# The queue that writes split weight parts back to memory: SyncE's, or GpSimd's where GpSimd makes the lo part

## The chip, the core and the metric

The kernel runs on one core of a Trainium2 chip. The metric is the device time of one execution in microseconds (us). Engines are named as in the profile: PE (TensorE matmuls), PEld (its weight loads), DVE (VectorE), ACT (ScalarE), POOL (GpSimd) and SP (SyncE, which here only issues DMAs). "SPq" is the queue of SP's instructions.

## What is computed

One layer of a decoder trunk over 2048 prompt tokens and 8 sample tokens of width 1024, in float32. Cut to its shape:

```python
h = rmsnorm(x, g_mix) * (1 + scale_m) + shift_m          # modulation from c @ w_ada
q, k, v, g_ret, x_lru, g_lru = split(h @ w_in)           # 1024 x 3072
ret_out = silu(g_ret) * norm(retention(rot(q), rot(k), v))
lru_out = rg_lru(causal_dwconv(x_lru)) * gelu(g_lru)
x = x + gate_m * (concat(ret_out, lru_out) @ w_out)      # 1024 x 1024
h = rmsnorm(x, g_ffn) * (1 + scale_f) + shift_f
u, gv = h @ w_up_conv, h @ w_up_gate                     # 1024 x 2816 each
x = x + gate_f * ((gelu(causal_dwconv(u)) * gv) @ w_down)  # 2816 x 1024
y = rmsnorm(x, g_final)
```

States of the retention, the recurrence and the two convolutions are outputs too.

## The kernel before

**Tiling.** The tokens are cut into three groups (688, 680 and 680 + 8), and each group into two blocks of 340 or 344 columns. A group runs through the layer's stages in turn: projection with retention and recurrence, output projection, then the up, gate and down products. The up and gate products are done for pairs of 128 output columns (pairs 0 to 10) with seven products for eight (`quad_item`), so their left operands are blocks of the weights (A11, A12, A22) or sums of them (S1 to S4).

**Split weights.** A float32 product is made of three fast ones: hi x hi, hi x lo and lo x hi (`mm3`, L373 to L375; only L375 reads a weight's lo part). So each weight block of 128 x 512 is split in a tile `wb` of 128 x 1024: ACT copies it rounded into the first half (L303), and POOL or DVE (`lo_on`, L304) subtracts that to fill the second. This is done when a key (a weight block's name) comes up for the first time. The whole tile, 512 KB, is then written to a DRAM tile `split[key]` (L310), and later groups read it back with one load (L301). Keys called `late` are not written the first time, but are split again in the second group and written then.

**Who makes lo.** `fetch(k, lo_on=V if near else G)`: DVE for the upper half of w_out and for pairs 0 to 2 of the up and gate weights, and for the first keys of the program; POOL for the others.

**Order and queues.** The main loop runs over a list of items (one product each) and fetches keys ahead until those that are not yet used weigh 4 (`LOOK`). A scheduler then fixes the order of each engine's instructions ahead of time, from its own model of their cost, and each engine works through its own list in order. Loads of raw weights (`wr`, L281 and L287) share a ring of 7 tiles with the sums `ws` (L357); the blocks `wb` share a ring of 8. In the kernel before, all of these loads and all writes are issued by SP. POOL issues 11 small loads at the start (L183, L246) and no other DMA; its work is lo parts of weights (L304) and of activations (`ffl`, `flast`, `mix`, L458), and small steps of the norms, the rotation and the recurrence. PE reads w_ada's raw tiles directly (L397).

Of the kernel before, what the change touches and what calls it, by code (L numbers as in the profile page):

```python
# [10 lines left out]
F32 = mybir.dt.float32  # L11
# [87 lines left out]
def hybrid_step(ctx: ExitStack, tc: tile.TileContext, I, O):  # L99
    nc = tc.nc  # L100
    V, S, G, T = nc.vector, nc.scalar, nc.gpsimd, nc.tensor
# [166 lines left out]
    split = {}  # L268
# [22 lines left out]
    def late(key):  # L291
        kind, a = key[0], key[1]
        if kind == "w_in":
            t = a // P
            return t % 4 == 3 or t >= 16 and t % 4 == 2 or t < 16 and t % 4 == 0
        return kind == "w_out" and a % 512 >= 2 * P

    def parts(key, w, src=None, lo_on=G):

        if src is None:  # L300
            nc.sync.dma_start(out=w.bitcast(F32), in_=split[key])  # L301
        else:
            S.activation(out=w[:, 0:512], in_=src, func=AF.Copy)  # L303
            lo_on.tensor_tensor(out=w[:, 512:1024], in0=src, in1=w[:, 0:512].bitcast(F32), op=ALU.subtract)  # L304
            nm = "_".join(str(v) for v in key)
            if late(key) and key not in once:
                once.add(key)
                return [w[:, 512 * i:512 * i + 512].rearrange("p (k c) -> p k c", c=P) for i in range(2)]
            split[key] = dp.tile([P, 1024], F32, tag=nm, name=nm)
            nc.sync.dma_start(out=split[key], in_=w.bitcast(F32))  # L310
        return [w[:, 512 * i:512 * i + 512].rearrange("p (k c) -> p k c", c=P) for i in range(2)]

    def fetch(key, r_=None, lo_on=G):

        kind, a = key[0], key[1]
        if kind == "ada01":
            src = I["w_ada"][0, key[2] * P:(key[2] + 1) * P, 0:2 * D].rearrange(
                "p (j c) -> p j c", j=2)[:, :, a * 512:(a + 1) * 512]
            if isinstance(r_, tuple):
                for j in range(2):  # L320
                    nc.sync.dma_start(out=r_[j], in_=src[:, j])
            else:
                nc.sync.dma_start(out=r_.rearrange("p (j c) -> p j c", j=2), in_=src)
                r_ = (r_[:, 0:512], r_[:, 512:1024])
            units[key] = [h[:, c:c + 256] for h in r_ for c in (0, 256)]
        elif kind == "w_ada":
            r_ = [load_rows_of(kind, key[2] * P, a * D + 512 * h) for h in range(2)]
            units[key] = [r_[h][:, c:c + 256] for h in range(2) for c in (0, 256)]
        elif kind in ("w_down", "w_out"):

            units[key] = parts(key, block(), None if key in split else load_rows_of(kind, a, 512 * key[2]), lo_on)
        elif kind == "w_in":
            both = []
            for h in range(2):
                r_ = None if key + (h,) in split else load_cols_of(kind, a, h)
                both.append(parts(key + (h,), block(), r_, lo_on))
            units[key] = [(both[k // 4][0][:, k % 4, :], both[k // 4][1][:, k % 4, :]) for k in range(KC)]
        else:
            fetch_operand(key, lo_on)

    def fetch_operand(key, lo_on):


        kind, i, nm = key
        if key in split:
            units[key] = parts(key, block())
            return
        pr = pairs.setdefault((kind, i), {})

        def A(n):  # L350
            if n not in pr:
                pr[n] = load_cols_of(kind, P * (2 * i + int(n[1]) - 1), int(n[2]) - 1)
            return pr[n]

        def total(n, x, y, op):
            pr[n] = rtile("ws")
            V.tensor_tensor(out=pr[n], in0=x, in1=y, op=op)  # L357

        if nm == "S1":
            total("S1", A("A21"), A("A22"), ALU.add)  # L360
            total("S2", pr["S1"], A("A11"), ALU.subtract)
        elif nm == "S2":
            total("S4", A("A12"), pr["S2"], ALU.subtract)
        elif nm == "S3":
            total("S3", A("A11"), A("A21"), ALU.subtract)
        units[key] = parts(key, block(), A(nm) if nm[0] == "A" else pr[nm], lo_on)
        if (i == 1 or i == 2 and kind == "w_up_conv") and nm in ("A11", "A12"):

            del pr[nm]
# [1083 lines left out]
```

## Time and profile before

| | |
|---|---|
| median of 3 runs | 2460.2 us (2459.76 to 2463.95) |
| the profiled execution | 2463.86 us, its span 2462.1 us |
| mean granted TensorE clock | 0.988 |
| SP's main queue (q1) | 532.01 MB, 62.6% of the 16 DMA engines' span |
| DMAs issued by POOL (q0) | 0.56 MB, 0.1% |
| weight blocks written (L310) | 262 of 512 KB each, all on SP |
| lo parts made by POOL (L304) | 228 |

The page gives busy times of the engines, the chain of work that ended last, and groups of instructions by line. A line number names the instruction's place in the kernel: L303 hi, L304 lo, L310 the write, L301 the load of a written block. A row "A <- B" of the view of waits says that engine A's instruction stood until B's ended. The stage views show the same numbers for stretches of the span.

### The profile page before, as it was taken

Reading aid. Unit: us, or ns where it says so; the run is one execution under the profiler, and the core shown is the slowest. Engines: PE = TensorE matmul, PEld = TensorE weight load, DVE = VectorE, ACT = ScalarE, POOL = GpSimd, SP = SyncE. Lnnn points to the kernel's source line nnn. Section 1 sums busy time; section 2 is a strip of 40 time slices with the busy share of each in tenths; the row PEclk is TensorE's granted clock in tenths of the full one; section 3 lists DMA queues with packets and bytes.
Section 4 is the critical chain, followed back from the end, with each engine's and each line's share of the span. In section 5 each row is a group of like instructions: output and inputs, shape, how many; then the busy total and the mean of one; then the engine's idle time right before and its main releaser. Section 6 shows DMA issues by size and latency. Waiting matters only on the chain.

```text
span 2462.1 us, 40114 instructions
## 1 busy us (share of the span) xinstructions
PE 2359.8 (96%) x15157; PEld 2275.5 (92%) x15157; DVE 1452.9 (59%) x3181; ACT 869.6 (35%) x1964; POOL 716.9 (29%) x739
## 2 busy tenths in 40 slices
PE   5999998999999999999899999999999989999998
PEld 4987797999999999999899999999999989999998
DVE  5646777875766665666754444446667675444444
ACT  4323554544444444243422222243124241222222
POOL 3444440257666743243001010112222210101011
PEclk9999999999999999999999999999999999999999
DMA  9476655878878875343566666666442465666674
GB/s 299 163 261 223 210 172 190 305 276 287 304 285 304 323 251 184 120 157 139 189 222 235 222 238 220 241 213 215 139 130 96 145 231 199 239 220 234 219 252 160
DMA packets 243493, 536.04 MB, mean 218 GB/s; under 512 B 19223, under 2 KB 114055, under 8 KB 243292
## 3 DMA queue, kind: packets, MB, share of 16 engines
q1 hardware_dynamic: 242220, 532.01, 62.6%
q8 instruction: 120, 1.97, 0.3%
q10 hardware_dynamic: 696, 0.91, 0.1%
q0 software_dynamic: 384, 0.56, 0.1%
q14 instruction: 73, 0.60, 0.1%
HBM read 385.10 MB, written 148.42 MB: 217 GB/s over the span
## 4 chain that ended last, share of the span: by engine, by line
PE 53%; DVE 4%; ACT 2%; DMA 1%; issue 1%; POOL 1%; POOLq 0%; SPq 0%; ACTq 0%; DVEq 0%
PE down L374 6%; PE down L373 6%; PE down L375 6%; PE qx L374 4%; PE qx L375 4%; PE qx L373 4%; PE proj L373 3%; PE proj L375 3%; PE proj L374 3%; PE qz L373 2%; PE qz L374 2%; PE qz L375 2%; PE qy L374 1%; PE qy L373 1%; PE qy L375 1%
## 5 line engine op out<-in xcount | busy, mean ns | idle before, releaser
L851 DVE SCALAR_TENSOR_TENSOR x<-down,mod,x 128x344 f32<-128x344 f32 (+2 forms) x624 | 349.0, 569 | 347.0 <-PE down L375 342.3
L373 PE MATMUL proj<-hh,wb 128*128 128x344 f32 (+1 forms) x1152 | 378.5, 329 | 14.3 <-DVE h L580 6.0
L375 PE MATMUL proj<-hh,wb 128*128 128x344 f32 (+1 forms) x1152 | 373.6, 325 | 2.7 <-POOL wb L304 2.5
L374 PE MATMUL proj<-hl,wb 128*128 128x344 f32 (+1 forms) x1152 | 372.5, 323 | 0.0
L458 POOL TENSOR_TENSOR ffl<-cv,ffh 128x344 fp32r<-128x344 f32 (+1 forms) x120 | 124.7, 1046 | 782.0 <-ACT ffh L457 736.7
L374 PE MATMUL qx<-op,wb 128*128 128x344 f32 (+1 forms) x1020 | 325.5, 319 | 2.6 <-DVE op L921 2.6
L373 PE MATMUL qx<-op,wb 128*128 128x344 f32 (+1 forms) x1020 | 324.7, 320 | 1.2 <-ACT op L920 1.2
L375 PE MATMUL qx<-op,wb 128*128 128x344 f32 (+1 forms) x1020 | 324.5, 319 | 0.0
L373 PE MATMUL down<-ffh,wb 128*128 128x344 f32 (+1 forms) x960 | 304.7, 324 | 7.6 <-DVE x L851 7.4
L375 PE MATMUL down<-ffh,wb 128*128 128x344 f32 (+1 forms) x960 | 306.4, 319 | 0.0
L374 PE MATMUL down<-ffl,wb 128*128 128x344 f32 (+1 forms) x960 | 306.3, 319 | 0.0
L304 POOL TENSOR_TENSOR wb<-wr,wb 128x512 fp32r<-128x512 f32 x164 | 223.9, 1376 | 230.7 <-ACT wb L303 222.1
L373 PEld LDWEIGHTS proj<-hh,wb 128*128 128x128 f32 x1152 | 218.4, 190 | 25.9 <-issue 9.5
L375 PEld LDWEIGHTS proj<-hh,wb 128*128 128x128 f32 x1152 | 218.7, 190 | 5.7 <-POOL wb L304 3.9
L374 PEld LDWEIGHTS proj<-hl,wb 128*128 128x128 f32 x1152 | 219.1, 190 | 3.3 <-POOL hl L588 0.9
L1076 DVE SCALAR_TENSOR_TENSOR cv<-u,vec,cv 128x344 f32<-128x344 f32 (+2 forms) x264 | 170.8, 665 | 50.6 <-ACT cv L1056 48.1
L374 PEld LDWEIGHTS qx<-op,wb 128*128 128x128 f32 x1020 | 191.7, 188 | 3.4 <-DVE op L921 3.4
L373 PEld LDWEIGHTS qx<-op,wb 128*128 128x128 f32 x1020 | 191.5, 188 | 2.0 <-ACT op L920 1.8
L373 PEld LDWEIGHTS down<-ffh,wb 128*128 128x128 f32 x960 | 179.3, 188 | 14.3 <-DVE x L851 13.7
L375 PEld LDWEIGHTS qx<-op,wb 128*128 128x128 f32 x1020 | 191.4, 188 | 0.0
L373 PE MATMUL qz<-op,wb 128*128 128x344 f32 (+1 forms) x528 | 169.7, 325 | 14.6 <-ACT op L920 10.7
L375 PEld LDWEIGHTS down<-ffh,wb 128*128 128x128 f32 x960 | 180.6, 188 | 0.0
(314 smaller groups left out, 4952.1 us busy)
## 6 DMA issues: line engine op xcount, KB each, us to landing
wb<-w_down SPq DMA_DIRECT2D x100, 512.0 KB
wb<-w_up_conv_S SPq DMA_DIRECT2D x92, 512.0 KB
wb<-w_up_gate_S SPq DMA_DIRECT2D x92, 512.0 KB
wb<-w_in SPq DMA_DIRECT2D x72, 512.0 KB
wb<-w_up_conv_A SPq DMA_DIRECT2D x69, 512.0 KB
wb<-w_up_gate_A SPq DMA_DIRECT2D x69, 512.0 KB
w_in<-wb SPq DMA_DIRECT2D x48, 512.0 KB
w_up_conv_S<-wb SPq DMA_DIRECT2D x44, 512.0 KB
```

The lines of the kernel that those rows point to most:

```text
L304: lo_on.tensor_tensor(out=w[:, 512:1024], in0=src, in1=w[:, 0:512].bitcast(F32), op=ALU.subtract)
L373: T.matmul(out, wh, xh, start=first, stop=False, skip_group_check=more)
L374: T.matmul(out, wh, xl, start=False, stop=False, skip_group_check=more)
L375: T.matmul(out, wl, xh, start=False, stop=last, skip_group_check=more)
L458: G.tensor_tensor(out=lo[:, 0:n], in0=src, in1=hi[:, 0:n].bitcast(F32), op=ALU.subtract)
L851: V.scalar_tensor_tensor(out=xs, in0=q[:, 0:np_], scalar=modv[:, jg, m, 0:1], in1=xs, op0=ALU.mult, op1=ALU.add)
L1076: V.scalar_tensor_tensor(out=cv[:, 0:np_], in0=u[:, j:j + np_], scalar=cfw[:, j, ft:ft + 1], in1=cv[:, 0:np_], op0=ALU.mult, op1=ALU.add)
```

## The change

```diff
             split[key] = dp.tile([P, 1024], F32, tag=nm, name=nm)
-            nc.sync.dma_start(out=split[key], in_=w.bitcast(F32))
+
+            (nc.gpsimd if lo_on is G else nc.sync).dma_start(out=split[key], in_=w.bitcast(F32))
         return [w[:, 512 * i:512 * i + 512].rearrange("p (k c) -> p k c", c=P) for i in range(2)]
```

The write of a split block is issued by POOL where POOL makes the lo part, and by SP as before where DVE makes it. The added blank line moves all lines behind it down by one: in the kernel after, the write is L311, `mm3` L374 to L376 and the activations' lo L459.

Of 262 writes, 212 move to POOL: 48 of w_in, 8 of w_out, 56 of w_up_conv, 56 of w_up_gate and 44 of w_down. The 50 others stay on SP. Since the scheduler places all instructions again, the order on the other engines moves too: PE's from its 428th row to the second group's projections, and not behind them (on ACT two small steps change places near the end).

The order on SP, in the projections of the first group (the place at 205 to 226 us of the profile before). `wr` are raw weight tiles, `w_in_0_2281` is the DRAM tile of a key's first half. Before:

```order
L287 DMA wr<-in_w_in 128x4x128 x2
L287 DMA wr<-in_w_up_conv 128x4x128
L310 DMA w_in_0_2281<-wb 128x1024
L281 DMA wr<-in_w_ada 128x512 x2
L310 DMA w_in_1_2288<-wb 128x1024
L310 DMA w_up_conv_S_2332<-wb 128x1024
L287 DMA wr<-in_w_in 128x4x128 x2
L281 DMA wr<-in_w_ada 128x512 x2
L310 DMA w_in_0_2347<-wb 128x1024
```

The same place in the change:

```order
L287 DMA wr<-in_w_in 128x4x128 x2
L287 DMA wr<-in_w_up_conv 128x4x128
L281 DMA wr<-in_w_ada 128x512 x2
L287 DMA wr<-in_w_in 128x4x128
L311 DMA w_up_conv_S_2332<-wb 128x1024
L287 DMA wr<-in_w_in 128x4x128
L281 DMA wr<-in_w_ada 128x512 x4
```

The loads keep their order. The three writes of w_in are gone from between them, and the write of w_up_conv's S, whose lo part DVE makes, stays and now stands between the two w_in loads.

The order on POOL, in the feed-forward of the first group (at 646 to 660 us of the profile before), where the lo parts of pair 6 and of w_down are made. Before:

```order
L304 TENSOR_TENSOR wb_7209<-wr_7185,wb_7209 128x512
L458 TENSOR_TENSOR ffl_7133<-cv_6845,ffh_7132 128x344
L304 TENSOR_TENSOR wb_7231<-ws_7229,wb_7231 128x512
L304 TENSOR_TENSOR wb_7236<-ws_7187,wb_7236 128x512
L458 TENSOR_TENSOR ffl_7158<-cv_6884,ffh_7157 128x344
L304 TENSOR_TENSOR wb_7249<-wr_7250,wb_7249 128x512
L458 TENSOR_TENSOR ffl_7182<-cv_6948,ffh_7181 128x344
L304 TENSOR_TENSOR wb_7286<-wr_7287,wb_7286 128x512
L304 TENSOR_TENSOR wb_7332<-wr_7107,wb_7332 128x512
L304 TENSOR_TENSOR wb_7369<-wr_7370,wb_7369 128x512
```

In the change, from three writes behind wb_7209 on:

```order
L311 DMA w_up_conv_6_S2_7192<-wb_7189 128x1024
L304 TENSOR_TENSOR wb_7231<-ws_7229,wb_7231 128x512
L304 TENSOR_TENSOR wb_7236<-ws_7187,wb_7236 128x512
L304 TENSOR_TENSOR wb_7249<-wr_7250,wb_7249 128x512
L311 DMA w_up_conv_6_A12_7212<-wb_7209 128x1024
L304 TENSOR_TENSOR wb_7286<-wr_7287,wb_7286 128x512
L311 DMA w_up_conv_6_S3_7234<-wb_7231 128x1024
L311 DMA w_up_conv_6_S4_7239<-wb_7236 128x1024
L311 DMA w_down_1280_1_7254<-wb_7249 128x1024
L304 TENSOR_TENSOR wb_7332<-wr_7107,wb_7332 128x512
L311 DMA w_down_1408_1_7291<-wb_7286 128x1024
L304 TENSOR_TENSOR wb_7369<-wr_7370,wb_7369 128x512
```

The lo parts keep their order; between wb_7209 and wb_7369 there are now eight writes (two of w_down stand ahead of the rows shown), one to three lo parts behind the part that they write.

The order on PE at the product that reads wb_7369 (the gate's A11 of pair 6), with its first lo matmul as the third row of that product. Before:

```order
L375 MATMUL qz_7214<-op_4274,wb_7236 128x344
L373 MATMUL qx_7490<-op_4006,wb_7369 128x344
L374 MATMUL qx_7490<-op_4006,wb_7369 128x344
L375 MATMUL qx_7490<-op_4006,wb_7369 128x344
L373 MATMUL qx_7490<-op_4006,wb_7369 128x344
L374 MATMUL qx_7490<-op_4006,wb_7369 128x344
L373 MATMUL down_7316<-ffh_7101,wb_7136 128x344
```

In the change:

```order
L375 MATMUL down_7467<-ffl_7182,wb_7286 128x344
L376 MATMUL down_7467<-ffh_7181,wb_7286 128x344
L374 MATMUL qx_7490<-op_4006,wb_7369 128x344
L375 MATMUL qx_7490<-op_4006,wb_7369 128x344
L374 MATMUL qz_7526<-op_4194,wb_7413 128x344
L375 MATMUL qz_7526<-op_4194,wb_7413 128x344
L374 MATMUL down_7475<-ffh_7101,wb_7249 128x344
```

The product starts 45 rows further back in PE's list, and its first lo matmul 83 rows further back, behind down products and a part of pair 6's A22 that stood after it before.

## The prediction

> **What bounds the kernel now.** The page's head and its chain of waits come first, then the busy time of the engines by stage. Columns of the stage rows: stretch in us, its length, busy time (and instructions) of PE, PEld, DVE, ACT and POOL, granted TensorE clock, share of the DMA engines, GB/s.
>
> ```profile
> span 2462.1 us, 40114 instructions
> PE 2359.8 (96%) x15157; PEld 2275.5 (92%) x15157; DVE 1452.9 (59%) x3181; ACT 869.6 (35%) x1964; POOL 716.9 (29%) x739
> PE 53%; DVE 4%; ACT 2%; DMA 1%; issue 1%; POOL 1%; POOLq 0%; SPq 0%; ACTq 0%; DVEq 0%
> 60.00:180.00 120.00, 120.00 (x808) 106.87 (x808) 64.54 (x179) 37.56 (x71) 52.77 (x59) 1.00 0.64 212
> 180.00:310.00 130.00, 120.58 (x771) 99.31 (x770) 90.20 (x165) 55.72 (x98) 58.13 (x58) 0.99 0.66 215
> 450.00:860.00 410.00, 400.00 (x2506) 392.40 (x2505) 283.08 (x421) 188.35 (x429) 254.46 (x195) 1.00 0.82 296
> 1260.00:1630.00 370.00, 370.00 (x2386) 369.94 (x2385) 159.83 (x305) 94.73 (x243) 37.16 (x38) 1.00 0.68 235
> ```
>
> TensorE is busy for 96% of the span, and no other engine has more than 4% of the chain. So a change to queues pays only where PE stands still for a weight. All the moved writes lie in group 0, apart from 24 of the late w_in keys, whose parts are made again and written in group 1. The stage rows show three kinds of stretch. From 60 to 180 us PE never stops (120.00 of 120.00), although the writes are already being made. From 180 to 310 us it stands still for 9.4 us. From 450 to 860 us, the feed-forward of group 0, where most of the writes lie, it stands still for 10 us of 410. The same work in group 1 (1260 to 1630 us), where split weights are only read back, has no gap.
>
> Next, what PE waited for in 180 to 310 us, and in 450 to 860 us (the last two rows). Columns: engine, line, waited for; total us, times, longest.
>
> ```profile
> PE proj L373 <- ACT wb L303: 2.9, 2, 1.9
> PE proj L375 <- POOL wb L304: 2.5, 2, 2.1
> PE zr L816 <- DVE xc L807: 2.5, 1, 2.5
> PE ada L397 <- DMA wr<-in_w_ada: 0.6, 2, 0.4
> PE down L373 <- ACT wb L303: 0.3, 1, 0.3
> PE down L373 <- DVE x L851: 7.4, 19, 1.6
> PE down L374 <- POOL flast L458: 1.6, 2, 0.9
> ```
>
> In 450 to 860 us PE waits for a PSUM bank that DVE has to drain (7.4 us), never for a weight part. Weights are late only in 180 to 310 us: 2.9 + 2.5 + 0.6 + 0.3 us, and the 2.5 us for the recurrence chain stand behind a late projection. The row for POOL's wb reads the same over the whole span, so the 24 writes of group 1 hold no PE wait either and count as 0.
>
> **What goes: writes that hold SP.** SP issues in order, so a load behind a write stands until the lo part is made. The waits of SP, over the whole span (first row) and in 180 to 310 us, and how long POOL's own DMA issues take by line (last three rows: instruction ns, min/median/max):
>
> ```profile
> SPq L310 <- POOL wb L304: 344.7, 155, 18.9
> SPq L281 <- DVE ws L357: 17.0, 3, 11.1
> SPq L281 <- PE ada L397: 16.3, 8, 4.6
> SPq L310 <- POOL wb L304: 16.1, 5, 4.9
> SPq L310 <- DVE wb L304: 8.0, 4, 2.8
> SPq L287 <- POOL wb L304: 6.9, 5, 2.5
> SPq L287 <- PE ada L397: 5.6, 2, 4.6
> SPq L281 <- POOL wb L304: 4.1, 3, 3.6
> L183 POOL DMA_DIRECT2D rows<-in_state_ffn_conv x3: 526/539/558, 4.5 to 5.5; - x3
> L246 POOL DMA_DIRECT2D wri<-in_w_r x2: 653/662/670, 6.1 to 6.7; - x2
> L183 POOL DMA_DIRECT2D rows<-in_conv_ffn_w x1: 772/772/772, 1.6 to 1.6; - x1
> ```
>
> The 344.7 us are the time for which SP stood at a write whose lo part POOL had not finished; these waits leave SP. Most of them hide nothing from PE, since the lo parts stand several products ahead. In 180 to 310 us the seven waits listed come to 74.0 us, of which the moved writes have 16.1, or 22%. The others stay: a load that waits for a slot of the seven raw tiles (for ws, ada or wb), and the writes whose lo part DVE makes (8.0 us), which remain on SP and stand in front of the same loads. The weight waits of PE with the recurrence are 8.8 us, and the clock of 0.99 over 130 us costs 1.3 us more, 10.1 us in all. The gain's upper end is therefore 10 us, if every one of them hangs on the writes, and its share by SP's waits is 22% of 10.1 = 2.2 us. I take **-2 us**, because one place can be followed on SP's timeline (start, length, engine, line, transfer) and PE's:
>
> ```profile
> 212.81 0.34 SPq L310 DMA_DIRECT2D w_in<-wb  x1
> 213.25 1.21 SPq L281 DMA_DIRECT2D wr<-in_w_ada  x2
> 215.08 0.38 SPq L310 DMA_DIRECT2D w_up_conv_S<-wb  x1
> 215.52 2.67 SPq L287 DMA_DIRECT2D wr<-in_w_in  x2
> 222.42 0.43 PE L373 MATMUL proj<-hh,wb 128*128 128x344 f32 x1 [1.03 <-ACT wb L303]
> ```
>
> The write at 212.81 is the one that SP waited for (longest 4.9 us); the w_in loads that PE lacks at 222.42 go out 2.7 us later. Without it they can move up, and this 1.0 us goes, but the write at 215.08 has a lo part from DVE and still stands between the two. Where this wait goes, the raw slots are late next. The other direction is open too: an lo part that PE takes at once (the two waits of 2.5 us) comes later by each write that POOL issues first. I allow one write ahead of each of the five waits for parts (2 + 2 + 1 times), 5 x 0.54 us, 3 us lost.
>
> The Trainium skill (DMA: Bandwidth & Descriptors, "Issuing engines are not separate DMA queues") says that transfers from any engine run on the same 16 DMA engines and that spreading the issue saves only sequencer time. Taken alone, that makes the change worth 212 issues on SP and nothing on PE, a term of 0 for my -2; the row of 344.7 us shows a wait in order that this rule does not count.
>
> **What comes: 212 issues on POOL.** POOL's own DMA issues are in the trace, in its first 9 us: 0.53 to 0.56 us for 128 rows, 0.65 to 0.67 for the larger pattern, 0.77 for the first. A write of a block has 128 rows, so I take **0.54 us**. All 212 cost 114 us of POOL, which has 1745 us free in the span. What counts is where they lie: 156 of them (44 of w_down, 112 of the up and gate operands of pairs 3 to 10) are in 450 to 860 us. There POOL goes from 254.5 to 254.5 + 84.2 = 338.7 us of 410, from 62% to 83%. It is not full, but its work comes in bursts, here on POOL's timeline, with the product that needs the last part:
>
> ```profile
> L304 POOL TENSOR_TENSOR wb<-wr,wb 128x512 fp32r<-128x512 f32 x90 | 125.8, 1411 | 89.2 <-ACT wb L303 84.7 <-DVE x L851 3.4 <-DMA wr<-in_w_in 0.9
> L304 POOL TENSOR_TENSOR wb<-ws,wb 128x512 fp32r<-128x512 f32 x64 | 91.2, 1431 | 56.4 <-ACT wb L303 45.2 <-DMA w_up_conv_A<-wb 11.1
> 649.85 2.83 POOL L304 TENSOR_TENSOR wb<-ws,wb 128x512 fp32r<-128x512 f32 x2
> 652.63 0.94 POOL L458 TENSOR_TENSOR ffl<-cv,ffh 128x344 fp32r<-128x344 f32 x1
> 653.51 1.30 POOL L304 TENSOR_TENSOR wb<-wr,wb 128x512 fp32r<-128x512 f32 x1
> 654.76 0.94 POOL L458 TENSOR_TENSOR ffl<-cv,ffh 128x344 fp32r<-128x344 f32 x1
> 655.64 4.26 POOL L304 TENSOR_TENSOR wb<-wr,wb 128x512 fp32r<-128x512 f32 x3
> 661.77 0.32 PE L375 MATMUL qx<-op,wb 128*128 128x344 f32 x1
> ```
>
> The last of the three at 655.64 is wb_7369 and ends at 659.90; its first lo matmul is the one at 661.77, so 1.87 us are to spare. In POOL's new order eight writes stand between wb_7209 and wb_7369: 8 x 0.54 = 4.3 us. In the old PE order that is 2.4 us late, and over the eight pairs 3 to 10 19 us: the upper end. But PE's order changes as well: that lo matmul is 83 rows further back, at 400 us / 2506 = 0.16 us each 13 us later, behind work on parts that are older. So I take **+1 us**, near the lower end of 0: no weight part was waited for in this stage, and in the two rows above POOL itself stands idle for 145.6 us at these parts, mostly for ACT's hi part, which the earlier loads can only bring forward. If that cover is gone the 19 us come. What is queued behind a write on POOL is the next lo part or the lo half of an activation (ffl), for which PE waits; the write itself waits for the lo part ahead of it on the same engine, and for its queue's eighth write before. Where that one has not landed, POOL stands; writes lie about 2.6 us apart (410/156), so eight are 21 us, against 6.5 to 7.7 us to landing:
>
> ```profile
> DMA to landing us min/median/max: 6.5/6.8/7.7
> L357 DVE TENSOR_TENSOR ws<-wr 128x512 f32<-128x512 f32 x37 | 39.5, 1067 | 61.5 <-DMA wr<-in_w_up_gate 51.2 <-POOL wb L304 9.6 <-DMA wr<-in_w_up_conv 0.6
> ```
>
> The first row is that of the four wri loads of POOL. The bytes moved are the same, and a block is written again only after PE has used it, so a write that lands a few us later delays no one at 0 us; its bound is the same 19 us.
>
> **The sum.** -2 + 1 = -1 us. The profiled execution took 2463.9 us (span 2462.1), 3.7 us over the median of the three timed runs, 2460.2; taken from its own time that is 2462.9, and a median run should again lie some 3.7 us lower. I forecast **2459 us**. A measurement of this kernel can tell about 0.2%, 4.9 us, from no change.
>
> **Rivals.**
> - *SP runs free*: all weight waits of 180 to 310 us go, with the clock: 2460.2 - 10 = 2450. For it speak the 344.7 us; against it, the 57.9 of 74.0 us of SP waits that stay there.
> - *POOL fills up* (slower): in 450 to 860 us a write holds POOL twice as long as in its quiet start, 1.08 us; 254.5 + 168.5 = 423 us do not fit into 410, and PE waits for lo parts: +13, 2473. It decides from 155.5 us free / 156 = 1.00 us per write on, and hurts earlier where bursts run over. For it: the lo parts there take 1411 and 1431 ns on average, so POOL is already slowed beside DVE. Against it: 0.54 against 1.00.
> - *DVE holds up POOL's DMA issues*: each write waits for one DVE instruction of 1.07 us before its 0.54; 156 x 1.61 = 251 us against 155.5 free, +96, 2556. The Trainium skill (SBUF — State Buffer, "SBUF: two separate sides") describes such a lock against descriptors made on GpSimd, for DVE instructions that use both ports on one source, 620 ns becoming about 3100. The row above is a two-input form, so I give it little.
> - *Nothing changes places*: SP only waits for raw slots instead, and POOL's issues hide: 2460, inside the forecast.
>
> **How the numbers follow.** Forecast with the last rival 0.48, SP free 0.26, POOL full 0.23, the lock 0.03. The forecast's own spread crosses 4.9 us once in fifty on either side: faster 0.26 + 0.01 = 0.27, same 0.46, slower 0.23 + 0.03 + 0.01 = 0.27. The range takes the ends of the terms, 2460.2 - 10 = 2450 and 2460.2 + 19 = 2479; the lock stays outside, and the forecast's own range is 2455 to 2465.
>
> **What would show it.** Right: SP's wait at L310 for POOL's wb is all but gone, its waits on raw slots (ws, ada) have grown; POOL's busy time is about 831 us, a write at 0.5 to 0.7 us; PE's weight waits of 180 to 310 us are 2 us fewer, and PE still waits for no lo part in 450 to 860 us. Wrong: a median issue near 1 us on POOL with PE waiting for POOL's wb (slower), or PE without weight waits from 180 to 310 us (faster).

## The result, and the profile after

| | before | after |
|---|---|---|
| median of 4 runs each | 2461.7 us (2459.8 to 2464.0) | 2501.5 us (2500.2 to 2504.8) |
| ratio after / before | | 1.0169, 95% interval 1.0155 to 1.0183 |
| span of the profiled execution | 2462.1 us | 2503.1 us |

The change costs 40 us. The forecast was 2459 us with a range up to 2479, so the time lies outside it, on the slower side.

The head of the page after:

```profile
span 2503.1 us, 40095 instructions
PE 2369.3 (95%) x15157; PEld 2283.1 (91%) x15157; DVE 1485.3 (59%) x3181; ACT 879.2 (35%) x1969; POOL 823.6 (33%) x951
```

POOL has 212 instructions and 107 us more than before, close to what was forecast. What was not forecast is DVE: the same 3181 instructions take 1485.3 us instead of 1452.9.

Four stages of the kernel after, each cut at the count of PE's matmuls that the kernel before reaches at 60, 180, 310, 450 and 860 us (columns as in the prediction):

```profile
60.60:187.30 126.70, 121.91 (x808) 106.86 (x808) 66.12 (x179) 37.39 (x73) 67.06 (x82) 0.98 0.62 208
187.30:312.00 124.70, 120.04 (x772) 100.93 (x771) 86.62 (x165) 53.51 (x95) 60.73 (x66) 0.99 0.63 207
312.00:455.30 143.30, 124.56 (x770) 119.78 (x770) 110.67 (x242) 76.54 (x168) 39.67 (x46) 0.96 0.60 202
455.30:903.30 448.00, 412.02 (x2507) 401.58 (x2506) 305.46 (x413) 190.82 (x428) 322.88 (x341) 0.97 0.74 266
```

The last row is the feed-forward of group 0. It took 410 us before and takes 448.0 for as many matmuls (2507, one more at an edge): 38 of the 40 us. PE stands still for 36.0 us instead of 10.0, and its matmuls take 412.0 us instead of 400.0, because the granted clock is lower (0.97 against 1.00): around six stops of 2.0 to 4.3 us the trace has stretches of 3.4 or 6.8 us at half the clock (0.50 in 621.0 to 624.4 us, for one). The stage before has no stop over 1.6 us and no such stretch. Of the rest, 60 to 180 us before takes 6.7 us more, 180 to 310 us takes 5.3 us less, 310 to 450 us 3.3 us more. Behind it, 860 to 1260 us takes 3.3 us less, and the feed-forward of group 1 takes the same 370 us.

What PE waits for in that stage after (the chief rows):

```profile
PE qz L374 <- ACT wb L303: 12.5, 9, 3.7
PE qx L374 <- ACT u L1017: 11.4, 5, 4.3
PE down L374 <- DVE x L852: 5.1, 7, 1.1
PE qx L374 <- ACT p L1017: 3.0, 1, 3.0
```

PE waits for no lo part of POOL, as the prediction said. It waits for hi parts of ACT and for PSUM banks that ACT drains, neither of which it waited for there by more than 0.2 us before. The reader should not stop at ACT: it is the last of a chain. The sums `ws` of the weight parts, which DVE makes, by line in the kernel before (instruction ns, min/median/max) and who waited for them (us, times):

```profile
L357 DVE TENSOR_TENSOR ws<-wr,ws x22: 676/694/1780, 214.5 to 827.5; 128x512 f32<-128x512 f32 x22
...
  ACT wb L303: 9.3, 10
```

The same view of the kernel after:

```profile
L358 DVE TENSOR_TENSOR ws<-ws,wr x22: 674/688/4280, 210.0 to 871.7; 128x512 f32<-128x512 f32 x22
L358 DVE TENSOR_TENSOR ws<-wr,ws x22: 675/1260/5545, 220.8 to 872.7; 128x512 f32<-128x512 f32 x22
...
  ACT wb L303: 41.6, 20
```

The shortest sums take 0.67 to 0.68 us in both kernels. Before, the longest took 1.8 us; after, 5.5 us, and ACT waits 41.6 us for sums instead of 9.3. Not only sums are held: the convolution steps of L1104 take up to 4.0 us and those of L1077 up to 3.7, against 1.6 and 1.7 before. One such place, on the timeline of the kernel after: the longest sum on DVE and the sum behind it, then POOL beside it.

```profile
609.65 5.54 DVE L358 TENSOR_TENSOR ws<-wr,ws 128x512 f32<-128x512 f32 x1
615.12 1.41 DVE L358 TENSOR_TENSOR ws<-wr 128x512 f32<-128x512 f32 x1
609.66 1.29 POOL L304 TENSOR_TENSOR wb<-ws,wb 128x512 fp32r<-128x512 f32 x1
610.91 0.91 POOL L459 TENSOR_TENSOR ffl<-cv,ffh 128x344 fp32r<-128x344 f32 x1
611.78 0.57 POOL L311 DMA_DIRECT2D w_up_conv_S<-wb  x1
612.37 0.94 POOL L459 TENSOR_TENSOR ffl<-cv,ffh 128x344 fp32r<-128x344 f32 x1
613.27 1.28 POOL L304 TENSOR_TENSOR wb<-wr,wb 128x512 fp32r<-128x512 f32 x1
614.51 1.47 POOL L459 TENSOR_TENSOR ffl<-cv,ffh 128x344 fp32r<-128x344 f32 x1
```

The sum stands while POOL works off four instructions and a write one behind the other at their own pace. The write at 611.78 does not let it in; only the instruction at 614.51 takes longer (1.47 us instead of 0.91 to 0.94), so the sum gets in there, beside an elementwise instruction. What comes of it, on the same timeline for ACT, SP and PE (in brackets the wait ahead of the instruction):

```profile
616.57 1.15 ACT L303 ACTIVATE wb<-ws 128x512 fp32r<-128x512 f32 x2 [3.74 <-DVE ws L358]
616.56 0.83 SPq L281 DMA_DIRECT2D wr<-in_w_down  x2
620.39 0.63 ACT L303 ACTIVATE wb<-wr 128x512 fp32r<-128x512 f32 x1 [2.67 <-DMA wr<-in_w_down]
620.92 0.44 ACT L1017 ACTIVATE u<-qx 128x344 f32<-128x344 f32 x1
617.77 0.42 PE L374 MATMUL qz<-op,wb 128*128 128x344 f32 x1 [1.81 <-ACT wb L303]
621.42 0.66 PE L374 MATMUL qx<-op,wb 128*128 128x344 f32 x1 [3.07 <-ACT u L1017]
```

ACT stands 3.74 us for the sums, and PE 1.81 us for the hi part made of one. The sums also hold raw tiles, so SP's next loads of w_down leave only at 616.56. ACT works in order and stands 2.67 us for that load, with the drain of a PSUM bank behind it, for which PE stands another 3.07 us. These 4.9 us of PE stand behind the held sum and the one queued behind it. How much of them would be left with two short sums is not shown: SP had waited for these tiles since before the hold.

For comparison the timeline of the kernel before, where a sum also starts just behind a lo part: it is let in behind that one part, and the next lo part waits for it (1.75 us instead of 1.28).

```profile
515.97 1.76 DVE L357 TENSOR_TENSOR ws<-wr 128x512 f32<-128x512 f32 x1
515.89 1.29 POOL L304 TENSOR_TENSOR wb<-ws,wb 128x512 fp32r<-128x512 f32 x1
517.14 1.75 POOL L304 TENSOR_TENSOR wb<-wr,wb 128x512 fp32r<-128x512 f32 x1
```

### The profile page after: what moved, and what is told of

It reads as the page before. It is cut to its first block, busy times and chain, and to the rows that moved or that the text cites. A ratio compares the mean times of both kernels' runs of the same rounds, so it can differ in the third digit from the quotient of the medians.

```text
span 2503.1 us, 40095 instructions
## 1 busy us (share of the span) xinstructions
PE 2369.3 (95%) x15157; PEld 2283.1 (91%) x15157; DVE 1485.3 (59%) x3181; ACT 879.2 (35%) x1969; POOL 823.6 (33%) x951
## 4 chain that ended last, share of the span: by engine, by line
PE 53%; DVE 4%; ACT 3%; DMA 2%; issue 1%; POOL 1%; POOLq 0%; SPq 0%; ACTq 0%; DVEq 0%
PE down L375 6%; PE down L374 6%; PE down L376 6%; PE qx L375 4%; PE qx L374 4%; PE qx L376 4%; PE proj L374 3%; PE proj L376 3%; PE proj L375 3%; PE qz L374 2%; PE qz L375 2%; PE qz L376 2%; PE qy L374 1%; PE qy L375 1%; PE qy L376 1%
## 5 line engine op out<-in xcount | busy, mean ns | idle before, releaser
L374 PE MATMUL proj<-hh,wb 128*128 128x344 f32 (+1 forms) x1152 | 379.1, 329 | 17.2 <-DVE h L581 6.0
L459 POOL TENSOR_TENSOR ffl<-cv,ffh 128x344 fp32r<-128x344 f32 (+1 forms) x120 | 125.1, 1050 | 776.2 <-ACT ffh L458 734.9
L376 PE MATMUL proj<-hh,wb 128*128 128x344 f32 (+1 forms) x1152 | 373.0, 324 | 1.2 <-POOL wb L304 1.1
L374 PE MATMUL qx<-op,wb 128*128 128x344 f32 (+1 forms) x1020 | 327.4, 322 | 16.4 <-ACT u L1017 11.4
L376 PE MATMUL qx<-op,wb 128*128 128x344 f32 (+1 forms) x1020 | 325.2, 320 | 0.0
L374 PE MATMUL down<-ffh,wb 128*128 128x344 f32 (+1 forms) x960 | 304.0, 323 | 7.1 <-DVE x L852 6.7
L376 PE MATMUL down<-ffh,wb 128*128 128x344 f32 (+1 forms) x960 | 306.1, 320 | 0.0
L374 PEld LDWEIGHTS proj<-hh,wb 128*128 128x128 f32 x1152 | 218.4, 190 | 27.6 <-issue 8.4
L376 PEld LDWEIGHTS proj<-hh,wb 128*128 128x128 f32 x1152 | 218.5, 190 | 3.8 <-POOL wb L304 2.0
L374 PEld LDWEIGHTS qx<-op,wb 128*128 128x128 f32 x1020 | 192.4, 189 | 20.5 <-ACT u L1017 13.3
L374 PE MATMUL qz<-op,wb 128*128 128x344 f32 (+1 forms) x528 | 171.3, 328 | 26.3 <-ACT wb L303 12.5
L376 PEld LDWEIGHTS qx<-op,wb 128*128 128x128 f32 x1020 | 192.1, 189 | 0.4 <-POOL wb L304 0.4
L1077 DVE SCALAR_TENSOR_TENSOR cv<-u,vec,cv 128x344 f32<-128x344 f32 (+2 forms) x264 | 167.0, 651 | 40.7 <-ACT cv L1057 38.5
L374 PEld LDWEIGHTS down<-ffh,wb 128*128 128x128 f32 x960 | 179.5, 188 | 11.2 <-DVE x L852 10.6
L303 ACT ACTIVATE wb<-wr 128x512 fp32r<-128x512 f32 x206 | 125.3, 625 | 175.1 <-DMA wr<-in_w_in 59.8
```

What stands on the lines that cost most here:

```text
L374: T.matmul(out, wh, xh, start=first, stop=False, skip_group_check=more)
L376: T.matmul(out, wl, xh, start=False, stop=last, skip_group_check=more)
L459: G.tensor_tensor(out=lo[:, 0:n], in0=src, in1=hi[:, 0:n].bitcast(F32), op=ALU.subtract)
L1077: V.scalar_tensor_tensor(out=cv[:, 0:np_], in0=u[:, j:j + np_], scalar=cfw[:, j, ft:ft + 1], in1=cv[:, 0:np_], op0=ALU.mult, op1=ALU.add)
```

## The experiments

Differences are to the median of the kernel before, measured beside it on the same chip. All edits are to `parts`, in the form of the changed line unless said. Every edit gives the scheduler a new order on all engines, which by itself can move the time by some us. The last two columns are from the trace of one run of each kernel: how long the feed-forward of group 0 takes, cut at the same counts of PE's matmuls as 450 and 860 us before, and how many of DVE's instructions in it take over 2 us.

| kernel | median, us | before, us | difference | stage, us | over 2 us |
|---|---|---|---|---|---|
| the kernel before | | | | 410.0 | 0 |
| the change | 2501.5 | 2461.7 | +39.8 | 448.0 | 18 |
| feed-forward's 156 writes on POOL | 2500.4 | 2460.8 | +39.6 | 450.8 | 17 |
| mixing stage's 56 writes on POOL | 2469.3 | 2460.0 | +9.3 | 406.6 | 0 |
| all 212 on ACT's queue | 2479.7 | 2460.8 | +18.9 | 416.2 | 0 |
| feed-forward's 156 on ACT's queue | 2469.8 | 2460.1 | +9.8 | 409.3 | 0 |
| writes on SP, 212 small DMAs on POOL | 2490.6 | 2460.0 | +30.6 | 434.7 | 20 |
| writes on SP, 67 small DMAs on POOL | 2486.3 | 2463.6 | +22.7 | 434.4 | 14 |
| writes on SP, POOL copies, 0.44 us per lo part | 2464.2 | 2460.8 | +3.4 | 412.0 | 0 |
| writes on SP, POOL copies, 0.55 us per lo part | 2468.4 | 2459.4 | +9.0 | 410.1 | 0 |
| writes on SP, POOL copies, 0.77 us per lo part | 2552.6 | 2463.6 | +89.0 | 488.0 | 0 |
| the change, and a small copy behind each write | 2549.3 | 2460.1 | +89.2 | 474.7 | 8 |
| the change with 9 raw tiles and 7 blocks | 2535.8 | 2460.0 | +75.8 | 477.4 | 22 |
| before with 9 raw tiles and 7 blocks | 2450.4 | 2460.1 | -9.7 | 399.1 | 0 |

Every kernel in which POOL issues DMAs among its work in that stage has instructions of DVE over 2 us there, and no other has one (the longest is 1.88 us).

### Where: the two parts of the change alone

```diff
+            (nc.gpsimd if lo_on is G and key[0] not in ("w_in", "w_out") else nc.sync).dma_start(...)
```

> Only the 156 writes of w_down, w_up_conv and w_up_gate are issued by POOL; the 56 of w_in and w_out stay on SP. By the place where PE fell behind (7 us at 150 to 180 us, some 38 us at 600 to 900 us), every theory expects 2492 to 2500; if it is the static order of the first group that the change spoiled, and not the issues themselves, the two losses need not come apart so: anything from 2455 to 2500.

Measured 2500.4 us, ratio 1.0158 (1.0129 to 1.0187). The loss of the feed-forward is that of its own writes, and the 7 us at 150 to 180 us are gone. The other part alone (`in ("w_in", "w_out")`):

> Only the 56 writes of w_in and w_out are issued by POOL; those of the feed-forward stay on SP. If the 7 us at 150 to 180 us belong to these writes and nothing else does: 2465 to 2470, with no loss in 450 to 900 us. If the place was an accident of the static order: 2455 to 2464.

Measured 2469.3 us, ratio 1.0029 (1.0013 to 1.0044). From 60 us on the 808 matmuls take 127 us as in the whole change (120 before). The first of PE's waits there:

```profile
PE ada L397 <- DMA wr<-in_w_ada: 2.8, 2, 2.5
```

So the 7 us at 60 to 180 us go with the writes of the mixing stage. The two parts do not add up: 39.6 + 9.3 is 49, the whole change costs 40.

### Without POOL's queue: the writes on ACT

```diff
+            (S if lo_on is G else nc.sync).dma_start(out=split[key], in_=w.bitcast(F32))
```

> The 212 writes are issued by ACT's queue instead of POOL's; POOL issues none. Theory 'late parts' (a write's 0.57 us on POOL pushes back the next lo part, so raw tiles come free later and loads start later): POOL has 0 us of writes, the loss of 40 us goes, 2455 to 2470, unless ACT's waits for lo parts hold its hi parts up. Theory 'held DVE' (DVE's two-operand instructions stand through a run of POOL instructions with DMA issues among them, up to 5.5 us instead of at most 1.8): no sum (L358) over 1.8 us, 2455 to 2470 under the same condition. Theory 'shared transfers' (writes on a queue of their own share the 16 DMA engines with the loads that PE needs next, instead of standing behind them on SP's queue): the loss stays, 2490 to 2505, with DVE's sums short.

Measured 2479.7 us, ratio 1.0074 (1.0045 to 1.0103), between all that was expected. No sum is over 1.8 us, here the largest group of them by line:

```profile
L357 DVE TENSOR_TENSOR ws<-wr x44: 673/693/1786, 182.6 to 839.1; 128x512 f32<-128x512 f32 x44
```

Half of the loss is left without a write on POOL's queue. Since part of it lay in 60 to 180 us again (128.4 us instead of 120), the feed-forward's writes were moved to ACT alone:

> The 156 writes of the feed-forward are issued by ACT's queue, the 56 of w_in and w_out by SP. What is left of the loss when no POOL instruction is a write and the mixing stage is as before: if held DVE sums are the main cause, 2462 to 2470 (ACT stands for lo parts, some 6 us in the run with all 212 on ACT); if the writes' leaving SP's queue costs by itself, 2475 or more.

Measured 2469.8 us (four runs from 2460.2 to 2475.3), ratio 1.0048 (1.0031 to 1.0065), at the upper end of the first case. By the median, 10 us of the feed-forward's 40 are lost without a write on POOL. Where they lie is not shown: the four runs differ by more than that, and the trace is that of the fastest, in which the stage takes no longer than before (columns as in the prediction):

```profile
450.20:859.50 409.30, 399.93 (x2506) 393.68 (x2505) 280.82 (x421) 190.48 (x429) 259.74 (x195) 1.00 0.83 300
```

ACT's own part, which waits in order for the lo parts that it writes, is in these 10 us and was not separated.

### Without moved writes: copies and small DMAs on POOL

```diff
             nc.sync.dma_start(out=split[key], in_=w.bitcast(F32))
+            if lo_on is G:
+                G.tensor_copy(out=junkw[:, 0:JW], in_=w[:, 512:512 + JW].bitcast(F32))   # JW = 144, bf16
```

> The writes stay on SP as before; POOL makes a copy of 128x144 behind each of the 212 lo parts, about as long as a write's issue (0.5 to 0.6 us expected), of no use to the result. 'Late parts': the same loss as with the writes on POOL, 2490 to 2505. 'Held DVE' by DMA issues: copies let DVE in between, no DVE sum over 2.3 us, 2460 to 2475. 'Shared transfers': 2460 to 2468.

Measured 2464.2 us, ratio 1.0018 (1.0002 to 1.0033). The copies came out shorter than a write: 0.44 us each, 93.6 us in all.

Next, the writes stay on SP and POOL issues something small that nobody reads:

```diff
             nc.sync.dma_start(out=split[key], in_=w.bitcast(F32))
+            if lo_on is G:
+                G.dma_start(out=dp.tile([P, 16], F32, tag="s" + nm, name="small"), in_=w[:, 512:528].bitcast(F32))
```

> All writes stay on SP as in the kernel before. Behind each of the 212 lo parts POOL issues one small DMA more (128 rows of 64 bytes, 8 KB, to a place that nobody reads). 'Held DVE' (a DMA issue among POOL's elementwise instructions keeps DVE from getting in between them): the loss comes back without any write moved, 2485 to 2505, with DVE sums of 3 to 5.5 us and PE behind in 600 to 900 us. If the loss came from the moved writes themselves (loads that SP sends earlier, transfers that share the DMA engines), 2460 to 2468 with no sum over 1.9 us.

Measured 2490.6 us, ratio 1.0129 (1.0112 to 1.0146). The groups of POOL by line (busy us, mean ns | idle before):

```profile
L312 POOL DMA_DIRECT2D small<-wb x212 | 117.7, 557 | 9.6 <-POOL wb L304 6.2 <-issue 3.4
```

And the sums, by line:

```profile
L359 DVE TENSOR_TENSOR ws<-wr,ws x22: 674/1101/5647, 214.0 to 851.4; 128x512 f32<-128x512 f32 x22
```

The sums are held, and three quarters of the loss come back with no write moved and only 1.7 MB more to transfer (212 x 8 KB). ACT waits 43.3 us for sums. But the DMAs take more of POOL than the copies did, 117.7 us against 93.6, so POOL's time could still be the cause. The next two runs set the two against each other. Two copies instead of one:

> Writes on SP as before, two copies of 128x144 on POOL behind each of the 212 lo parts: by the run with one copy (441 ns each, 93.6 us in all) some 0.6 to 0.9 us per lo part, more than a write's 0.57. 'Late parts' with a threshold (POOL's time per lo part decides: 0.44 cost 3 us, 0.56 about 31 to 40, 0.83 in the run with a write and a small copy 89): 2495 to 2550. 'Held DVE': POOL is fuller but lets DVE in, no sum over 2.3 us, 2460 to 2475.

Measured 2552.6 us, ratio 1.0357 (1.0339 to 1.0374): enough time on POOL does cost much. The copies took 162.9 us (424 of 384 ns), and PE waits for POOL's lo parts in the feed-forward, here the chief row, with no instruction of DVE over 1.8 us:

```profile
PE qx L378 <- POOL wb L304: 11.5, 7, 1.9
```

Fewer small DMAs (`and len(split) % 3 == 0`, 67 of them):

> Writes on SP as before, a small DMA of 8 KB on POOL's queue behind every third written block whose lo part POOL makes (about 70 instead of 212): 0.19 us per lo part on average. 'Late parts': less than the one copy's 0.44 that cost 3 us, so 2458 to 2466. 'Held DVE': a hold lasts until POOL's next DMA or idle time, so fewer issues make fewer but longer holds: sums over 3 us, 2470 to 2495.

Measured 2486.3 us, ratio 1.0094 (1.0078 to 1.0109), with 37.9 us on POOL (67 of 566 ns), less than the single copies took. The sums, by line:

```profile
L359 DVE TENSOR_TENSOR ws<-wr x44: 675/779/5936, 174.2 to 845.5; 128x512 f32<-128x512 f32 x44
```

Each theory was right in one of the two runs (the two copies came out 3 us over its range), so both costs are real. The last run sets POOL's time to that of the small DMAs, without a DMA (one copy of 128x144 behind every lo part, one of 128x16 behind half of them):

> Writes on SP, POOL without DMA issues: a copy of 128x144 behind each of the 212 lo parts and one of 128x16 behind about half of them, 0.53 to 0.57 us per lo part by the earlier runs (0.44, and half of 0.2 to 0.26), as long as a write's issue. If POOL's time per lo part makes the loss, it is lost here too: 2490 to 2505. If held DVE instructions make the larger part of it, 2462 to 2475; what is lost here is then the share of POOL's time.

Measured 2468.4 us, ratio 1.0036 (1.0024 to 1.0047). The groups of POOL by line:

```profile
L312 POOL CAST junkw<-wb 128x144 bf16<-128x144 f32 x212 | 83.6, 394 | 6.6
L314 POOL CAST junkw<-wb 128x16 bf16<-128x16 f32 x106 | 33.4, 315 | 2.2
```

And the largest group of sums, by line:

```profile
L361 DVE TENSOR_TENSOR ws<-wr x44: 673/701/1876, 173.0 to 831.8; 128x512 f32<-128x512 f32 x44
```

83.6 + 33.4 = 117.0 us on POOL against 117.7 for the small DMAs, behind the same lo parts: 9.0 us lost instead of 30.6. The other 22 us are what the DMAs cost beyond their time on POOL, and the run with 67 DMAs lost 23. The feed-forward of group 0 with small DMAs (first row) and with the copies (second; columns as in the prediction):

```profile
443.50:878.20 434.70, 406.33 (x2506) 396.72 (x2505) 322.93 (x418) 190.27 (x432) 316.39 (x341) 0.98 0.77 274
447.70:857.80 410.10, 398.00 (x2505) 391.61 (x2504) 281.10 (x421) 191.21 (x429) 324.92 (x409) 1.00 0.82 291
```

With copies POOL is as busy as in the change (324.92 us against 322.88), DVE takes no longer than in the kernel before (283.08), and the stage loses nothing. With DMAs DVE takes 40 us more and the stage 25. The two traces are of the faster runs of their kernels, 2464.0 and 2484.6 us.

### The hold by itself

These three kernels compute nothing of the layer. In the first, DVE makes 32 sums in each stretch:

> Nothing of the layer is computed: six stretches of 32 DVE sums of 128x512 (L127, L130, L134, L139, L144; L148 has one operand and a constant) beside POOL that does nothing (L127), lo parts (L130), lo parts and writes on its own queue (L134), lo parts with the writes on SP (L139), writes alone (L144), lo parts and writes beside one-operand DVE work (L148). 'Held DVE': L127 0.69 us; L130 and L139 at most about 1.8 us; L134 with single sums of 3 to 5.5 us; L144 open; L148 unaffected at its own length. The other theories: L134 like L139.

The sums by line, beside an idle POOL, lo parts, lo parts with writes on POOL, lo parts with writes on SP, and POOL writes alone:

```profile
L127 DVE TENSOR_TENSOR x<-x,y x32: 691/693/693, 14.6 to 37.1; 128x512 f32<-128x512 f32 x32
L130 DVE TENSOR_TENSOR x<-x,y x32: 691/1632/1635, 39.0 to 87.8; 128x512 f32<-128x512 f32 x32
L134 DVE TENSOR_TENSOR x<-x,y x32: 691/693/9132, 94.5 to 134.9; 128x512 f32<-128x512 f32 x32
L139 DVE TENSOR_TENSOR x<-x,y x32: 692/1632/1634, 166.8 to 210.0; 128x512 f32<-128x512 f32 x32
L144 DVE TENSOR_TENSOR x<-x,y x32: 691/693/693, 252.1 to 274.7; 128x512 f32<-128x512 f32 x32
```

Lo parts alone make a sum wait for one of them, 1.63 us; writes alone do nothing to it, 0.69 us; both together on POOL hold one sum of the 32 for 9.1 us. The same lo parts with the writes on SP do not. One-operand work (L148) was expected to be unaffected and was not: 0.43 us alone, up to 2.76 beside lo parts and writes.

> Nothing of the layer is computed: DVE makes sums of 128x512 all along, POOL repeats a pattern: one write of 64 KB and 1 lo part (DVE's L132), 2 (L140), 4 (L148), 8 lo parts (L156), two writes and 4 lo parts (L164), a copy of 128x144 and 4 lo parts without a write (L173), a write, a copy and 4 lo parts (L181). 'Held DVE', as far as the first measurement shows it (9.1 us with five lo parts and a write inside): a sum that starts beside a write stands until the next write, so the longest is about 2.5 us in L132, 3.2 in L140, 5.7 in L148 and L164, 10.7 in L156, and 1.63 in L173 as with lo parts alone. If the 9.1 us were a single accident, all stay at about 1.63.

The longest sums were 3.53 us (one lo part per write; the order put two lo parts and two writes together), 2.99 (two), 5.42 (four), 10.29 (eight) and 6.80 (two writes and four lo parts); a copy in the place of the write left them at 1.63, and a write, a copy and four lo parts gave 6.13. Eight lo parts per write on the timeline, POOL and then DVE:

```profile
206.69 9.79 POOL L160 TENSOR_TENSOR wb<-z,wb 128x512 fp32r<-128x512 f32 x8
216.43 0.56 POOL L157 DMA_DIRECT2D s<-wb  x1
206.74 29.72 DVE L156 TENSOR_TENSOR x<-x,y 128x512 f32<-128x512 f32 x3
```

Three sums in 29.72 us: the first two stand through eight lo parts each and the third through seven. The lo parts run at 1.22 us each as if DVE were not there, and the first two sums get in where POOL issues its next write. In these patterns a hold grows with the number of elementwise instructions between two writes. But a write does not always end it: the hold of 9.1 us above had a write inside, as had the 5.54 us in the kernel, and beside two writes and four lo parts some sums got in after 4.33 us at a lo part, with no write near. That a third of the DMAs costs almost as much as all fits fewer and longer holds (14 instructions of DVE over 2 us instead of 20, the longest 5.94 us instead of 5.65), but was not tested further.

> Nothing of the layer is computed: DVE makes sums of 128x512, POOL repeats a write and 4 lo parts (DVE's L132), the same with a copy of 128x16 right behind the write (L140), the same with a copy behind each lo part (L149). L132 repeats 5.4 us. If any other instruction of POOL's elementwise kind ends the hold, L140 falls to about 1.7 us; if only the copy itself lets DVE in, L140 stays near 5.4 (four lo parts with no copy among them) and L149 falls to about 1.7 to 2.2.

A write and four lo parts repeated 5.42 us. A copy right behind the write left it at 5.54, a copy behind each lo part brought it to 1.79. So a copy between lo parts lets DVE in where it stands, and one right behind the write does not prevent the hold. In the kernel the change with a copy behind each write:

> The changed kernel with a copy of 128x16 on POOL behind each of its 212 writes (some 0.27 us each, 57 us of POOL in all). If such a copy ends the hold, DVE's sums stay under 2.3 us and most of the loss in 600 to 900 us goes: 2465 to 2480 (the 7 us of the mixing stage stay, POOL is fuller). If it doesn't, or POOL is then too full: 2495 to 2515.

Measured 2549.3 us, ratio 1.0363 (1.0343 to 1.0384), slower than either case expected. The longest sum is 3.7 us instead of 5.5, but a write and a copy are about 0.83 us of POOL per lo part, and the loss is as large as that of the two copies (0.77 us). This was no remedy.

### Rings, and a faster kernel

```diff
-LOOK, RAWS, RING = 4, 7, 8
+LOOK, RAWS, RING = 4, 9, 7
```

> The changed kernel with 9 raw tiles instead of 7, and 7 blocks instead of 8 (the memory allows no more). If held DVE sums reach PE through raw tiles that come free late, two more of them cover a hold of 4 us: 2462 to 2480. If they reach it through ACT, which works in order and stands at the hi part of a late sum with the drain of a PSUM bank behind it, the loss stays: 2490 to 2505. A block less may cost something by itself.

> The kernel before (writes on SP) with 9 raw tiles and 7 blocks, the counterpart of the changed kernel with the same rings (2535.8). If the two raw tiles cover nothing of the hold, that pair differs by about 40 us as the original pair does: 2490 to 2500. If they cover it, the block less accounts for all: 2525 to 2540.

Measured 2535.8 us with the change (ratio 1.0308, 1.0288 to 1.0329) and 2450.4 us without it (0.9965, 0.995 to 0.998). Both expectations were wrong for both kernels: the first is slower than either case, the second faster. More raw tiles cover nothing of the change's loss, which is 85 us in this pair (75.8 + 9.7). In the slower one PE waits for DVE itself (waits of PE in the feed-forward):

```profile
PE down L373 <- DVE x L851: 39.2, 15, 4.7
```

DVE works in order too: the longest sum there stands from 537.13 us on for 6.36 us with the drains of down products behind it, and PE's next down product starts at 544.03 after 4.73 us of waiting for one. Why the loss is twice that of the change was not settled. The kernel before with these rings is the fastest of the study, 9.7 us under the kernel before; in its feed-forward PE is busy for 406.8 of 410 us instead of 400.0.

## Why the prediction was wrong

**The step that failed is the term of the feed-forward of group 0, "+1 us", upper end 19.** It counted what a write costs on POOL and who waits for POOL. That part was right: a write took a median 0.57 us (0.54 forecast, from the loads that POOL issues at the start, which are 12 and not 11), POOL's busy time in the stage rose by 68.4 us (84.2 forecast), and PE waited for no lo part. The step left out what a write does to DVE. It took a lo part and a sum to share as before, at the 1.07 us of the row of `ws`, and asked only whether DVE delays POOL. The runs show the other direction: DMAs that POOL issues among its lo parts hold DVE's sums and convolution steps, at 22 us by the medians and 25 us of the stage in the traces. POOL itself gains by it: its lo parts take 1368 and 1351 ns on average there instead of 1411 and 1431. The same 117 us of POOL time without DMAs cost 9 us by the median and nothing in the stage's trace, so the burst term itself stayed below its upper end of 19.

A rest of the stage's 38 us, some 13 (448.0 against 434.7), comes only with the large writes on POOL; it may be less, since the trace with small DMAs is of a run 6 us under its median. The prediction had no term for it, and what makes it is open. That it is the writes' leaving SP's queue is not shown: with writes on ACT's queue the stage took 416.2 us in one trace and 409.3 in the other.

By the medians, 22 + 9 + 10 = 41 come near the 39.6 of the feed-forward's writes. That is no proof: the runs have different orders, and by the stage's traces the parts are 25, nothing and the open 13.

**60 to 180 us, counted as 0:** wrong by 6.7 us. It goes with the writes of w_in and w_out wherever they are issued besides SP, and DVE is not held there (the run on ACT loses 8 us there). PE waited there for loads of w_ada, but whether the new static order or the loads' landing makes them late was not settled.

**180 to 310 us, -2 us:** right in the waits. The weight waits fell from 6.3 us to 2.1 + 1.1 + 1.0 + 0.4 = 4.6, by 1.7. The stretch is 5.3 us shorter, since the 2.5 us for the recurrence went too, and the next gives 3.3 of it back; that the two come to -2 again is luck, since nothing was forecast for the next.

**"SP no longer stands at writes, raw tiles are late next":** right. SP's waits for POOL at the write are gone, and its waits for raw tiles are now, over the whole span (the same four rows came to 75.9 us before):

```profile
SPq L287 <- POOL wb L304: 146.9, 57, 16.0
SPq L287 <- DVE ws L358: 142.8, 21, 17.1
SPq L281 <- POOL wb L304: 119.8, 40, 18.7
SPq L281 <- DVE ws L358: 113.7, 15, 20.4
```

344.7 us of waiting at one place became some 450 us more at another, and PE gained at most the 5.3 us of one stretch from it.

**The rivals.** "SP runs free" did not happen, and "Nothing changes places" was right about SP and wrong about POOL. "POOL fills up" had the right side, but its price rested on a write of 1.08 us, and a write takes 0.57; two copies (0.77 us per lo part) show that this cliff exists, at more POOL time than the change adds. "DVE holds up POOL's DMA issues" named the right pair of engines with the wrong one waiting. The Trainium skill (SBUF — State Buffer, "SBUF: two separate sides") says that a DVE instruction with two SBUF inputs contends with a GpSimd instruction that reads SBUF, and that the one that comes second waits for the other's whole instruction. The trace agrees for one instruction (1.63 us beside lo parts); a sum of 10.29 us beside eight of them goes beyond it. The prediction used that page for POOL's waiting alone.

## What to carry to other kernels

Where GpSimd does elementwise work beside two-operand work of VectorE, a DMA on GpSimd's queue can cost more than its issue, as it did here: look for the longest duration of VectorE's instructions, not the mean, and at the engine behind them. Writes that stand in a queue for a result of GpSimd can be almost free, as the 344.7 us were here, when what they hold back would stand for a buffer anyway. Before a queue is changed for such a wait, follow what the loads behind it would wait for next.

## What the runs showed of the hardware

- Beside POOL's elementwise instructions, a two-operand sum of 128x512 on DVE takes 1.63 us instead of 0.69. Once POOL has issued a DMA among them, a sum can stand through several of them: 10.29 us with eight lo parts between two DMAs. In fixed patterns it got in at the next DMA or a copy; in the kernel one of 5.54 us went past a write and got in at an elementwise instruction. DMAs of 8 KB do it in the kernel as those of 512 KB do.
- POOL's DMA issues alone, without elementwise work, do not slow a sum at all (0.693 us median and longest).
- What in POOL or its way to memory makes the hold was not tried; the runs show when it comes, and only in part when it ends.
